# The last quarter of an MLP's second product, done as seven half-size products

## The chip, the cores and the metric

The kernel runs on one core of one Trainium2 chip. The time is that of the device, in microseconds, from one launch of the whole program: two layers of an encoder, each with a token mixer and an MLP. Only the MLPs are changed.

A core has a matrix engine (TensorE; PE in the profile, with its weight loads listed apart as PEld), a vector engine (DVE), a scalar engine (ACT), GpSimd (POOL), and a queue that issues transfers (SP). POOL can issue transfers too. Each engine works through its own list of instructions in order and waits on semaphores where it needs another engine's result. SBUF is the on-chip memory; PSUM is where TensorE writes.

## What is computed

The input is 512 tokens of 1024 float32 values. After each token mixer comes

```python
def _sq_relu_mlp(h, w1, w2):
    a = jax.nn.relu(jnp.matmul(h, w1))
    return jnp.matmul(a * a, w2)

x = _layernorm(DEEPNORM_ALPHA * x + _sq_relu_mlp(x, w1[i], w2[i]), ln2_g[i], ln2_b[i])
```

with `w1` 1024 x 4096 and `w2` 4096 x 1024, all float32. Layer 0 has a gated DeltaNet mixer in front of its MLP, layer 1 a gated linear attention mixer; layer 1's MLP writes the output.

## The kernel before

**Precision.** TensorE is used with operands rounded to a shorter format (`F32R`). Each float32 operand is split into a high part (a rounding copy on ACT, line 95) and a low part (source minus high part, on DVE, line 96). Every product is then three matmuls, high x high, high x low and low x high (`mm3`, lines 114 to 116). So a split of a block costs one ACT and one DVE operation, and a product of 128 x 128 by 128 x 512 costs three matmuls.

**Groups.** The MLP's 4096 hidden features are worked in four groups of 1024. The first product makes a group's hidden activations `h`, the second multiplies them with the group's 1024 rows of `w2` and adds the result to `x` (tiles `xt`, four of 128 tokens, each seen as two halves of 512 columns). While TensorE does the second product of group g, pieces of the first product of group g + 1 (`nxt()`) are placed between its parts, so that both kinds of matmul share the engine's list.

**Seven products.** For groups 0 to 2, function `second` (line 469) cuts the product into 2 x 2 blocks: tokens into two halves of 256, hidden features into two halves of 512 (`a11`, `a12`, `a21`, `a22`), and `w2` into four blocks of 512 x 512. A scheme of the Strassen-Winograd kind gives the result with seven block products in place of eight. Each of the seven is 24 matmuls (two token tiles, four slices of features, three matmuls each). It costs sums: of activation blocks on DVE, of weight blocks on DVE (`plus`, line 348), and more adds of PSUM banks into `x` (line 464), since some products go into two results. The `w2` blocks arrive in raw form in a ring of 8 tiles (`w2r`, 128 x 1024); their split parts live in rings of 3 (`w2h`, `w2l`), those of the activations in rings of 2 (`ah`, `al`).

**The last group.** Group 3 has no next group to mix with. Function `last` (line 539) does its second product plainly: eight `w2` pieces are loaded and split (`rows`), four blocks of activations are split (`part`), and then for each of the four token tiles and each half of the columns 8 x 3 matmuls go into one PSUM bank (`pl`), 192 matmuls in all. As soon as both halves of a token tile are added to `x`, its layernorm runs (`layernorm`, line 214; its `last=True` keeps all of it on DVE but for two tiny ACT operations). In layer 0 the tile is then transposed and split for the next mixer (`xpose`, line 168); in layer 1 it is stored to the output.

`layernorm` has a second form, with `sums`: row sums come from the adds into `x` themselves, the squares from two ACT operations (line 219), and with `last=False` one half of the final scaling goes to ACT (line 233) and POOL (line 234). The kernel before uses it only after the token mixers.

**Order.** The program is written in the order in which the work is meant to run; a framework places the instructions of each engine, inserts the semaphores and orders each engine's list by its own estimates of when operands are ready. The order is fixed when the program is built. A ring tile is given out again only when all its readers are done, so ring sizes and the order of use also bind the engines to each other.

Of the kernel before, what the change touches and what calls it, by code (L numbers as in the profile page):

```python
# [17 lines left out]
P = 128  # L18
# [10 lines left out]
class Ctx:  # L29
# [52 lines left out]
        return self.psum[tag].tile(list(shape), dt, name=name, tag=tag)  # L82


    def split(self, src, shape, pool=None):

        nc = self.nc
        if pool is None:
            hi = self.whl.tile(shape, F32R, name="wh", tag="wh")
            lo = self.whl.tile(shape, F32R, name="wl", tag="wl")  # L90
        else:
            pool, hi, lo, bufs = pool
            hi = pool.tile(shape, F32R, name=hi, tag=hi, bufs=bufs)
            lo = pool.tile(shape, F32R, name=lo, tag=lo, bufs=bufs)
        nc.scalar.copy(hi, src)  # L95
        nc.vector.tensor_tensor(lo, src, hi.bitcast(F32), ALU.subtract)  # L96
        return hi, lo

    def wcols(self, w, c0, n=P, pool=None):
# [202 lines left out]
def mlp(c, w1, w2, g, b, out=None, extra=None):  # L302
# [14 lines left out]
    with c.banks(pj=2, X=2, Y=2, Z=2), tc.tile_pool(name="mlp", bufs=2) as pool:  # L317
# [5 lines left out]
        def ring(name):  # L323
            return (pool, *RING[name])
# [8 lines left out]
        def load(gi, i, j):  # L333
            for q in range(2):
                blocks[i, j, q] = t = raw()
                r = (gi * GF + i * HF + 2 * q) * P
                c.dma(t, w2[r:r + 2 * P, 512 * j:512 * j + 512].rearrange("(k p) n -> p k n", p=P))

        def split(i):

            i_, j_ = {1: (0, 0), 2: (1, 0), 3: (1, 1), 4: (1, 0), 5: (0, 0), 6: (0, 0), 7: (0, 1)}[i]
            parts[i] = [c.split(blocks[i_, j_, q], [P, 2, 512], pool=ring("w2")) for q in range(2)]

            sums = {1: ((0, 0), (0, 1)), 2: ((0, 1), (1, 1)), 5: ((0, 0), (1, 1)), 6: ((1, 0), (0, 0))}
            if i in sums:
                plus(*sums[i])

        def plus(a, b):
# [106 lines left out]
        def pair(src, where="ah"):  # L455
            return c.split(src, [P, HF, HT], pool=ring(where))

        def add(t, hf, ps, op=ALU.add):
            xs = c.xh(t)[hf]
            if (t, hf) not in touched:  # L460
                touched.add((t, hf))
                V.scalar_tensor_tensor(xs, xs, ALPHA, ps, ALU.mult, op)
            else:
                V.tensor_tensor(xs, xs, ps, op)

        def quarters(h):
            return [h[j][:, :, HT * i:HT * i + HT] for i in range(2) for j in range(2)]

        def second(gi, h, a, nxt):

            a11, a12, a21, a22 = quarters(h)

            def banks(tag):
                return [c.bank([P, 512], F32, name="p" + tag, tag=tag) for _ in range(2)]

            def product(bk, a, i, new, by_tile=False):

                if i not in parts:
                    split(i)
                ws = parts.pop(i)  # L480
                order = [(q, j) for j in range(2) for q in range(2)] if by_tile else [(q, j) for q in range(2) for j in range(2)]
                for q, j in order:
                    wh, wl = ws[q]
                    sl = slice(j * P, (j + 1) * P)
                    for k in (2 * q, 2 * q + 1):
                        c.mm3(bk[j], a[0][:, k, sl], a[1][:, k, sl], wh[:, k % 2, :], wl[:, k % 2, :],
                              new and k == 0, k == HF - 1, skip_group_check=True)

            def fetch(i, j):
                if gi + 2 < G:  # L490
                    load(gi + 1, i, j)

            X, Y = banks("X"), banks("Y")
            load(gi, 1, 0)
# [32 lines left out]
                add(j, 1, Y[j], ALU.subtract)  # L527
            nxt()
            if gi + 2 == G:
                nxt()  # L530
                nxt()
            product(X, pair(a22), 4, False)
# [3 lines left out]
                nxt()  # L536
                nxt()

        def last(gi, h):

            par = c.load_ln(g, b, lambda i: pool.tile([P, 512], F32, name="ln", tag=("xh5", "xh6", "xl5", "xl6")[i], bufs=1))
            a, ws = {}, {}

            def part(i, j, home):
                a[i, j] = pair(h[j][:, :, HT * i:HT * i + HT], home)

            def rows(i, home=None):
                ws[i] = c.wrows(w2, (gi * GF + 2 * (i % 4)) * P, i // 4 * 512, pool=ring(home) if home else None)

            rows(0)  # L550
            rows(3, "w2")
            part(0, 0, "ah")
            rows(1)
            rows(2)
            part(0, 1, "raw")
            rows(4, "raw")
            rows(5, "raw")
            rows(6, "w2")
            rows(7, "w2")
            part(1, 0, "ah")  # L560
            part(1, 1, "raw")
            if out is None:
                c.new_x()
            for t in range(NT):
                sl = slice(t % 2 * P, t % 2 * P + P)
                for hf in range(2):
                    ps = c.bank([P, 512], F32, name="pl", tag="YZYZXZXZ"[2 * t + hf])
                    for k in range(GF):
                        wh, wl = ws[4 * hf + k // 2]
                        ah, al = a[t // 2, k // HF]  # L570
                        c.mm3(ps, ah[:, k % HF, sl], al[:, k % HF, sl], wh[:, k % 2, :], wl[:, k % 2, :], k == 0, k == GF - 1)
                    add(t, hf, ps)
                c.layernorm(c.xh(t), c.xh(t), par, last=True)
                if out is None:
                    c.xpose(t, c.xt[t], ("pj",))
                else:
                    nc.sync.dma_start(out[t * P:(t + 1) * P, :], c.xt[t])
# [31 lines left out]
        early = {}  # L609
        step = 0  # L610
        for gi in range(G - 1):
            more = gi + 2 < G
# [24 lines left out]
            second(gi, h, a, nxt)  # L637
            h, a = nh, nxt.a if more else None
        last(G - 1, h)


def sel_masks(c, pool, tmp):
# [992 lines left out]
```

## Time and profile before

| | us |
|---|---|
| median of 3 runs | 1374.56 (1373.52 to 1374.7) |
| the profiled execution | 1370.78 |
| its span in the trace | 1369.1 |
| TensorE busy (8317 matmuls) | 1341.5 |
| DVE busy | 1073.9 |
| ACT busy | 738.7 |
| POOL busy | 72.5 |
| last group of layer 0, first to last `pl` matmul | 721.8 to 769.9 |
| last group of layer 1, first to last `pl` matmul | 1315.5 to 1360.0 |

Rows of the profile read: start in us from the span's start, length in us, engine, line, operation, names (`out<-in`), shape, and in brackets the engine's idle time before it with what ended it. Group rows carry a count (x), total busy us and mean ns of one. Rows of windows give, for each engine, the busy time and the count of instructions within the stretch, then the granted TensorE clock, the share of DMA time and GB/s. Matmuls are pipelined: one shown with 0.39 us is followed by the next after about 0.23. Numbers behind tile names are left out, so `w2r<-w2r` is a sum of two weight blocks.

### The profile page before, as it was taken

The numbers are of one execution on the slowest core, as the hardware profiler recorded it, in microseconds if no ns is written. First come the engines' busy times: TensorE is split into PE (matmuls) and PEld (weight loads), VectorE is DVE, ScalarE is ACT, GpSimd is POOL, SyncE is SP. The second block draws the span as 40 slices with busy tenths as digits, with TensorE's granted clock in tenths as the row PEclk, the third lists the DMA queues.
The fourth block names the chain that finished last, engine by engine and source line by source line (L and its number), as shares of the span: only waits on it lengthen the run. The fifth ranks groups of instructions, "written<-read, shape, count | busy, mean of one in ns | idle before, by whom it ended". The sixth has DMA issues, their size and how long they took to land.

```text
span 1369.1 us, 21146 instructions
## 1 busy us (share of the span) xinstructions
PE 1341.5 (98%) x8317; PEld 1123.9 (82%) x8317; DVE 1073.9 (78%) x1685; ACT 738.7 (54%) x1444; POOL 72.5 (5%) x111
## 2 busy tenths in 40 slices
PE   8999999999999999999999999999999999999997
PEld 7777777777777888888887888888878888888886
DVE  7787787778677997897967687977779787979675
ACT  4776668765743655555553354654446455545440
POOL 5000000000003700000000000000000000000000
PEclk9999999999999999999999999999999999999999
DMA  6221112210251523243123332221325153322141
GB/s 190 63 62 48 47 32 63 60 35 32 78 154 57 176 78 108 77 154 93 47 90 100 91 92 76 62 62 62 99 55 185 47 154 92 124 78 60 47 152 49
DMA packets 145222, 117.44 MB, mean 86 GB/s; under 512 B 6571, under 2 KB 121379, under 8 KB 145123
## 3 DMA queue, kind: packets, MB, share of 16 engines
q1 hardware_dynamic: 143779, 111.90, 27.2%
q0 software_dynamic: 1344, 4.20, 1.1%
q8 instruction: 65, 1.06, 0.3%
q14 instruction: 34, 0.28, 0.1%
HBM read 113.99 MB, written 2.10 MB: 85 GB/s over the span
## 4 chain that ended last, share of the span: by engine, by line
PE 83%; ACT 7%; DVE 6%; DMA 2%; issue 1%; POOL 0%; DVEq 0%; SPq 0%; ACTq 0%
PE pj L115 5%; PE pj L116 5%; PE pj L114 5%; PE pX L114 3%; PE pX L115 3%; PE pX L116 3%; PE pjv L114 3%; PE pjv L115 3%; PE pjv L116 3%; PE fxz L114 2%; PE scp L865 2%; PE op L1561 2%; PE fxz L115 2%; PE fxz L116 2%; PE pl L115 2%; PE pl L116 2%
## 5 line engine op out<-in xcount | busy, mean ns | idle before, releaser
L95 ACT CAST wh<-wst 128x1024 fp32r<-128x1024 f32 x146 | 152.8, 1050 | 203.8 <-PE pj L115 49.8
L96 DVE TENSOR_TENSOR wl<-wst,wh 128x1024 fp32r<-128x1024 f32 x146 | 178.9, 1232 | 62.2 <-ACT wh L95 62.1
L115 PE MATMUL pj<-xtl,wh 128*128 128x512 f32 (+1 forms) x352 | 127.1, 361 | 0.5 <-DVE xtl L178 0.5
L114 PE MATMUL pj<-xth,wh 128*128 128x512 f32 (+1 forms) x352 | 126.8, 362 | 0.8 <-ACT xth L177 0.7
L116 PE MATMUL pj<-xth,wl 128*128 128x512 f32 (+1 forms) x352 | 126.7, 361 | 0.0
L96 DVE TENSOR_TENSOR w2l<-w2r,w2h 128x1024 fp32r<-128x1024 f32 x84 | 102.5, 1222 | 26.6 <-ACT w2h L95 26.5
L95 ACT CAST w2h<-w2r 128x1024 fp32r<-128x1024 f32 x84 | 88.2, 1050 | 64.5 <-PE pX L116 28.1
L114 PEld LDWEIGHTS pj<-xth,wh 128*128 128x128 f32 x352 | 66.2, 189 | 11.2 <-ACT xth L177 1.2
L115 PEld LDWEIGHTS pj<-xtl,wh 128*128 128x128 f32 x352 | 66.4, 189 | 10.9 <-DVE xtl L178 0.8
L115 PE MATMUL pX<-w2l,ah 128*128 128x512 f32 x192 | 75.0, 391 | 0.0
L116 PE MATMUL pX<-w2h,al 128*128 128x512 f32 x192 | 74.9, 390 | 0.0
L114 PE MATMUL pX<-w2h,ah 128*128 128x512 f32 x192 | 74.8, 393 | 0.0
L116 PEld LDWEIGHTS pj<-xth,wl 128*128 128x128 f32 x352 | 66.4, 189 | 10.2
L95 ACT CAST ah<-h 128x1024 fp32r<-128x1024 f32 x46 | 48.4, 1053 | 46.8 <-PE pX L115 20.8
L351 DVE TENSOR_TENSOR w2r<-w2r 128x1024 f32<-128x1024 f32 x48 | 58.1, 1233 | 0.3
L96 DVE TENSOR_TENSOR al<-h,ah 128x1024 fp32r<-128x1024 f32 x46 | 56.2, 1221 | 0.6
L114 PE MATMUL pjv<-wh,xth 128*128 128x512 f32 x128 | 54.7, 427 | 0.0
L116 PE MATMUL pjv<-wh,xtl 128*128 128x512 f32 x128 | 50.2, 392 | 0.0
L115 PE MATMUL pjv<-wl,xth 128*128 128x512 f32 x128 | 50.0, 390 | 0.0
L116 PEld LDWEIGHTS pX<-w2h,al 128*128 128x128 f32 x192 | 36.1, 188 | 7.5
L116 PE MATMUL pjk<-xth,wl 128*128 128x512 f32 (+1 forms) x112 | 41.8, 373 | 0.0
L114 PEld LDWEIGHTS pX<-w2h,ah 128*128 128x128 f32 x192 | 35.8, 188 | 7.1 <-ACT w2h L95 0.3
(469 smaller groups left out, 3915.4 us busy)
## 6 DMA issues: line engine op xcount, KB each, us to landing
wst<-in_mlp_w SPq DMA_DIRECT2D x80, 512.0 KB, 4.3
w2r<-in_mlp_w SPq DMA_DIRECT2D x48, 512.0 KB, 3.7
wst<-in_a_w_in SPq DMA_DIRECT2D x32, 512.0 KB, 4.1
wst<-in_b_w_in SPq DMA_DIRECT2D x32, 256.0 KB, 3.0
wst<-in_a_w_out SPq DMA_DIRECT2D x8, 512.0 KB, 3.8
wst<-in_b_w_in SPq DMA_DIRECT2D x8, 512.0 KB, 3.8
wst<-in_b_w_out SPq DMA_DIRECT2D x8, 512.0 KB, 3.6
xt<-in_x SPq DMA_DIRECT2D x4, 512.0 KB, 4.1
```

Of the source, the lines that this page charges most:

```text
L95: nc.scalar.copy(hi, src)
L96: nc.vector.tensor_tensor(lo, src, hi.bitcast(F32), ALU.subtract)
L114: mm(ps, ah, bh, start=start, stop=False, **kw)
L115: mm(ps, ah, bl, start=False, stop=False, **kw)
L116: mm(ps, al, bh, start=False, stop=stop, **kw)
L351: V.tensor_tensor(blocks[a + (q,)], blocks[a + (q,)], blocks[b + (q,)], ALU.add)
L865: T.matmul(ps[:, n, :], kh[:, sl], qh[:, sl], start=True, stop=True)
L1561: T.matmul(op[:, n, :], l, r, start=i == 0, stop=i == len(mm) - 1)
```

## The change

Group 3 is now done with the seven products too. `last` takes the split first block of activations `a`, as `second` does, and runs the products in the order 1, 5, 2, 6, 3, 7, 4, with nothing between them. Three things differ from `second`:

- The sums of weight blocks are no DVE operations. `plus` issues transfers from POOL that read one raw tile in SBUF and add it to another (`accum_op=ALU.add`), 128 x 1024 each, two for each of four sums: eight per layer.
- Of each weight block's two halves, the first (q = 0) is split as before. The second gets tiles of its own (`xh3`/`xl3` and `xh7`/`xl7`, free since the first product's last use), and its low part is computed on POOL. That holds for products 2 to 7 of the group; product 1's halves are split on ACT and DVE ahead of time.
- The layernorm of token tiles 0 to 2 uses the `sums` form. That of tile 3 uses the old form in layer 1 and the `sums` form in layer 0. The output is stored in halves of 512 columns. Products 3, 7 and 4 finish one token tile before they start on the other (`by_tile`), and in layer 0 the transposes of tiles 0 and 1 stand within product 4 (`behind`).

Around it: the first block of group 3 is split within group 2's loop (`split(1)`), `w2` of group 3 is fetched within group 2's products (`fetch` without its condition), and group 2's product 4 is split before the last two pieces of the first product instead of after. POOL's instructions within `last` are held in the order in which they are written (`in_order`). `banks` and `product` move out of `second` unchanged but for the `behind` hook.

```diff
-    def split(self, src, shape, pool=None):
+    def split(self, src, shape, pool=None, lo_on=None):
...
-        nc.vector.tensor_tensor(lo, src, hi.bitcast(F32), ALU.subtract)
+        (lo_on or nc.vector).tensor_tensor(lo, src, hi.bitcast(F32), ALU.subtract)
...
-        def split(i):
+        def split(i, homes=None):
...
-            parts[i] = [c.split(blocks[i_, j_, q], [P, 2, 512], pool=ring("w2")) for q in range(2)]
+            parts[i] = [c.split(blocks[i_, j_, q], [P, 2, 512], *((homes if homes and q else (ring("w2"),))))
+                        for q in range(2)]
...
-                plus(*sums[i])
+                plus(*sums[i], homes)
...
-                V.tensor_tensor(blocks[a + (q,)], blocks[a + (q,)], blocks[b + (q,)], ALU.add)
+                if by_dma:
+                    nc.gpsimd.dma_start(blocks[a + (q,)], blocks[b + (q,)], accum_op=ALU.add)
+                else:
+                    V.tensor_tensor(blocks[a + (q,)], blocks[a + (q,)], blocks[b + (q,)], ALU.add)
...
             if gi + 2 == G:
+                split(4)
                 nxt()
                 nxt()
...
-        def last(gi, h):
+        def last(gi, h, a):
+            homes = {i: ((pool, f"xh{k}", f"xl{k}", 1), nc.gpsimd) for i, k in ((5, 3), (2, 7), (6, 3), (3, 7), (7, 3), (4, 7))}
+            a11, a12, a21, a22 = quarters(h)
...
+            def full(t, hf, ps, sign=1.0):
+                xs = c.xh(t)[hf]
+                V.scalar_tensor_tensor(xs, ps, sign, xs, ALU.mult, ALU.add, accum_out=sums[t][:, hf:hf + 1])
+
+            def norm(t, end):
+                if end and out is not None:
+                    c.layernorm(c.xh(t), c.xh(t), par, end)
+                else:
+                    junk = pool.tile([P, HF, S], F32, name="h", tag="h", bufs=3)
+                    c.layernorm(c.xh(t), c.xh(t), par, end, (sums[t], (junk[:, 0, :], junk[:, 1, :])))
+                if out is not None:
+                    for q in range(2):
+                        nc.sync.dma_start(out[t * P:(t + 1) * P, 512 * q:512 * q + 512], c.xh(t)[q])
...
+            load(gi, 1, 0)
+            X, Y = banks("Z"), banks("Y")
+            V.tensor_tensor(a21, a22, a21, ALU.subtract)
+            a5 = pair(a21)
+            split(5, homes[5])
+            product(X, a, 1, True)
+            for j in range(2):
+                add(j, 0, X[j])
+            a2 = pair(a12)
+            split(2, homes[2])
+            product(Y, a5, 5, True)
+            V.scalar_tensor_tensor(a11, a21, -1.0, a11, ALU.mult, ALU.subtract)
+            V.scalar_tensor_tensor(a21, a11, -1.0, a22, ALU.mult, ALU.subtract)
+            for j in range(2):
+                add(2 + j, 1, Y[j], ALU.subtract)
+            a6 = pair(a11)
+            split(6, homes[6])
+            Z = banks("X")
+            product(Z, a2, 2, True)
+            V.scalar_tensor_tensor(a12, a12, -1.0, a11, ALU.mult, ALU.subtract)
+            for j in range(2):
+                full(j, 0, Z[j])
+            a3 = pair(a12)
+            split(3, homes[3])
+            product(X, a6, 6, False)
+            for j in range(2):
+                add(j, 1, X[j], ALU.subtract)
+            a7 = pair(a21)
+            split(7, homes[7])
+            product(Y, a3, 3, False, True)
+            for j in range(2):
+                full(j, 1, Y[j], -1.0)
+            a4 = pair(a22, "raw")
+            split(4, homes[4])
+            product(X, a7, 7, False, True)
+            for j in range(2):
+                full(2 + j, 1, X[j], -1.0)
+            norm(0, False)
+            norm(1, False)
+            product(X, a4, 4, False, True, turn)
+            for j in range(2):
+                full(2 + j, 0, X[j])
+                norm(2 + j, j == 1)
+            turn(2)
+            turn(3)
...
-                if half == 1 and i % 4 == 2 and more:
-                    split(1)
+                if half == 1 and i % 4 == 2:
+                    split(1, None if i + 2 < len(todo) else (None, None))
                     nxt.a = pair(quarters(nh)[0])
...
-        last(G - 1, h)
+        with c.in_order(mybir.EngineType.Pool):
+            last(G - 1, h, a)
```

The lines numbered in the prediction are those of the kernel before, except line 556, which is the `scalar_tensor_tensor` within `full` of the changed kernel.

More of the change, by code (lines that the diff above doesn't have):

```diff
@@ L537, in second @@
                 nxt()
-        def last(gi, h):
+        def last(gi, h, a):
+            homes = {i: ((pool, f"xh{k}", f"xl{k}", 1), nc.gpsimd) for i, k in ((5, 3), (2, 7), (6, 3), (3, 7), (7, 3), (4, 7))}
+            a11, a12, a21, a22 = quarters(h)
             par = c.load_ln(g, b, lambda i: pool.tile([P, 512], F32, name="ln", tag=("xh5", "xh6", "xl5", "xl6")[i], bufs=1))
[L542 to L561, printed above, removed]
+            sums = [c.small.tile([P, 2], F32, name="lns", tag="lns") for t in range(NT)]
@@ L562, in last @@
             if out is None:
                 c.new_x()
[L564 to L573, printed above, removed]
+            def full(t, hf, ps, sign=1.0):
+                xs = c.xh(t)[hf]
+                V.scalar_tensor_tensor(xs, ps, sign, xs, ALU.mult, ALU.add, accum_out=sums[t][:, hf:hf + 1])
@@ L574, in last, with turn @@
+            def turn(t):
                 if out is None:
                     c.xpose(t, c.xt[t], ("pj",))
-                else:
-                    nc.sync.dma_start(out[t * P:(t + 1) * P, :], c.xt[t])
+            load(gi, 1, 0)
[7 more added lines that the diff above has]
+            a2 = pair(a12)
@@ L611, in mlp @@
         for gi in range(G - 1):
-            more = gi + 2 < G
             nh = new_h()
```

35 lines of the change are left out of this document (18 added, 17 removed).

## The prediction

> **What bounds the kernel now.** I read the page first (busy shares and the chain that ended last), then the stretch of the second layer's last group by windows, then the timelines of PE and DVE there.
>
> ```profile
> PE 1341.5 (98%) x8317; PEld 1123.9 (82%) x8317; DVE 1073.9 (78%) x1685; ACT 738.7 (54%) x1444; POOL 72.5 (5%) x111
> ...
> PE 83%; ACT 7%; DVE 6%; DMA 2%; issue 1%; POOL 0%; DVEq 0%; SPq 0%; ACTq 0%
> ```
>
> TensorE is busy nearly always and carries 83% of the chain; GpSimd (POOL) is almost unused. The windows show the second layer before its last group, then that group's first 11 us and the rest of its matmuls:
>
> ```profile
> 1280.00:1315.00 35.00, 35.00 (x194) 30.43 (x193) 19.86 (x25) 16.79 (x23) 2.15 (x4) 1.00 0.32 107
> 1315.00:1326.00 11.00, 10.74 (x46) 8.13 (x45) 10.12 (x10) 8.12 (x10) 0.00 (x0) 1.00 0.38 139
> 1326.00:1360.00 34.00, 33.64 (x148) 27.89 (x149) 20.36 (x42) 1.50 (x6) 0.00 (x0) 1.00 0.11 47
> ```
>
> Behind the stretch and its length stand the busy times of PE, the weight loads, DVE, ACT and POOL. PE is full. DVE is full only for the 11 us in which the splits are made; it works 19.9 of the 35 us before and 20.4 of the 34 after. So fewer matmuls pay one for one, as long as what replaces them fits on DVE.
>
> ```profile
> 1256.63 0.39 PE L114 MATMUL pY<-w2h,ah 128*128 128x512 f32 x1
> ...
> 1261.85 0.39 PE L116 MATMUL pY<-w2h,al 128*128 128x512 f32 x1
> ...
> 1315.51 0.39 PE L114 MATMUL pl<-wh,ah 128*128 128x512 f32 x1
> ...
> 1326.36 0.50 PE L115 MATMUL pl<-w2l,w2r 128*128 128x512 f32 x1 [0.61 <-DVE w2l L96]
> ```
>
> The first two rows are the ends of one seven-product product of 24 matmuls: (1261.85 - 1256.63) / 23 = 0.227 us each, so 5.45 us a product. The last two are the group at stake: its first matmul at 1315.51 (called T0 below) and its one wait, of 0.61 us.
>
> **The change part by part.**
>
> *Matmuls.* 192 become 7 x 24 = 168. 24 x 0.227 = 5.45 us a layer, and the wait of 0.61 goes with its order: -6.1 us in each of two layers, all of it on PE's path.
>
> *What DVE has to do instead.* Each product needs a split of its own weight block and of its own activations. In the built program's order DVE has, between the finished activations and the add that frees product 4's bank (line 556 for token tile 2): 16 operations of 128x1024 on two SBUF tiles (four sums of activation blocks, six low parts of activations, six of weights), 13 adds of a PSUM bank into x, and the first part of tile 0's layernorm.
>
> ```profile
> 1318.57 0.68 DVE L464 TENSOR_TENSOR xt<-xt,pX 128x512 f32<-128x512 f32 x1
> 1319.17 1.22 DVE L96 TENSOR_TENSOR w2r<-wst,w2r 128x1024 fp32r<-128x1024 f32 x1
> 1320.30 1.22 DVE L96 TENSOR_TENSOR al<-h,ah 128x1024 fp32r<-128x1024 f32 x1
> ...
> 1329.52 0.75 DVE L226 SCALAR_TENSOR_TENSOR xt<-xt,bmv,ln 128x512 f32<-128x512 f32 x1
> ...
> 1330.92 0.15 DVE L189 SCALAR_TENSOR_TENSOR rst<-bmv,rst 128x1 f32<-128x1 f32 x1
> ```
>
> By the distance of the starts a 128x1024 operation costs 1.13 us and a PSUM add 0.60. 16 x 1.13 = 18.1; 13 x 0.60 = 7.8; the layernorm part is three operations of 128x512 like line 226 (0.7 from start to start) and seven of one column (0.15): 3.2. Together 29.1 us, while PE needs 6 x 5.45 = 32.7 us to reach product 4. That alone would fit.
>
> *GpSimd's half of the low parts.* Six 128x1024 subtractions go to POOL. The trace shows what such an operation does to DVE:
>
> ```profile
> 21.73 1.29 POOL L1073 TENSOR_TENSOR off<-blk 128x512 f16<-128x512 f32 x1
> ...
> 423.81 1.71 POOL L234 TENSOR_TENSOR xt<-xt,lnp 128x512 f32<-128x512 f32 x1 [27.80 <-ACT xt L233]
> 427.23 1.27 POOL L234 TENSOR_TENSOR xt<-xt,lnp 128x512 f32<-128x512 f32 x1 [1.71 <-ACT xt L233]
> ```
>
> ```profile
> 21.75 2.35 DVE L96 TENSOR_TENSOR wl<-wst,wh 128x1024 fp32r<-128x1024 f32 x1
> ...
> 423.62 0.74 DVE L231 SCALAR_TENSOR_TENSOR xt<-xt,rstd,lnp 128x512 f32<-128x512 f32 x1
> 424.28 1.26 DVE L189 SCALAR_TENSOR_TENSOR rst<-bmv,rst 128x1 f32<-128x1 f32 x1
> ...
> 427.10 0.68 DVE L178 TENSOR_TENSOR xtl<-tp,xth 128x512 fp32r<-128x512 f32 x1
> ```
>
> The split at 21.75 began 20 ns after a POOL operation of 1.29 us and took 2.35 in place of 1.22: it lost 1.13 us, all but 0.16 of POOL's time. At 423.81 POOL had to wait for line 231 (1.71 in place of 1.27), and then a one-column DVE operation waited for POOL (1.26 us in place of 0.15). The line 178 operation, with one operand in PSUM, ran beside POOL at its usual 0.68. So in this trace POOL and a DVE operation on two SBUF tiles exclude each other for the whole operation, and PSUM adds are exempt.
>
> ```profile
> L1083 POOL TENSOR_TENSOR ic<-ic 128x64 f32<-128x64 f32 x1 | 0.3, 324 | 0.1
> ```
>
> From 324 ns at 64 columns to 1.27 us at 512, undisturbed, is 2.11 ns a column: 2.35 us at 1024, an estimate. Each then takes 2.35 - 0.16 = 2.2 us from DVE, twice what DVE would need for the same split. Five of the six fall into the stretch counted above: 11.0 us. A pair of adds beneath one hides 1.2. Bounds for DVE's work: 29.1 + 11.0 - 5 x 1.2 = 34.1 with adds beneath all five, 40.1 with none. In the built order adds stand next to some of them, and I take two covered: 37.7. DVE also waits for ScalarE, whose casts and squares feed it in order: I add 2 us, three of the squares below, with 0 to 3 as bounds. Work starts when the last activation is squared:
>
> ```profile
> 1315.67 0.63 ACT L450 ACTIVATE h<-h 128x512 f32<-128x512 f32 x1
> ```
>
> This ended at T0 + 0.8; with two weight casts fewer ahead of it I expect it 2 us earlier, and after the first POOL operation DVE starts at about T0 - 1.5. So the add of tile 2 ends at -1.5 + 37.7 + 2 = T0 + 38.2, and PE, due at T0 + 32.7, has lost 5.5 us (bounds -0.1, which is nothing, and 8.9), spread over the products as late low parts. The matmuls saved are given back here.
>
> *Product 4's second half, and the tail (layer 1).* The add for tile 3 stands on DVE behind tile 1's layernorm and a POOL addition of 128x512 (3.2 + 1.27 against the 2.7 us of a half product): 1.2 us of waiting, 0 to 2. At the end DVE still holds most of tile 2's layernorm when PE finishes, where before only tile 3's was left:
>
> ```profile
> 1360.46 0.69 DVE L464 TENSOR_TENSOR xt<-xt,pl 128x512 f32<-128x512 f32 x1 [4.02 <-PE pl L116]
> ```
>
> Then it waited 4.02 us for PE; now PE's end finds it busy. Tile 2's 3.2 us and one POOL addition fall between, less what has run by then: +2.3 (0.5 to 4). Storing in halves saves perhaps 0.2, within that.
>
> *Layer 0.* The same -6.1 + 5.5. Transposes of tiles 0 and 1 fill product 4's wait, but the layernorms of tiles 1 to 3 follow the last matmul instead of one, and the next token mixer's first projection waits for them:
>
> ```profile
> 771.14 0.36 PE L114 MATMUL pjq<-xth,wh 128*128 128x256 f32 x1 [0.87 <-DVE xt L464]
> ```
>
> Before, that wait was 0.87 us because other tokens came first. I take two layernorm parts and one POOL addition on PE's path, less 2.7 us of work that it has meanwhile: 2 x 3.2 + 1.27 - 2.7 = +5.0 (1 to 7).
>
> *Accumulating transfers.* Eight per layer stand for what would be eight sums on DVE. No row shows an accumulating transfer.
>
> ```profile
> w2r<-in_mlp_w SPq DMA_DIRECT2D x48, 512.0 KB, 3.7
> ...
> wst<-in_b_w_in SPq DMA_DIRECT2D x32, 256.0 KB, 3.0
> ...
> lnp<-in_ln_b POOLq DMA_DIRECT2D x2, 256.0 KB, 3.4
> ```
>
> ```profile
> DMA to landing us min/median/max: 3.3/5.2/7.4
> ```
>
> 256 KB more cost 0.7 us on SP's queue, so 512 KB move in 1.4 of 3.7; POOL's queue adds 0.4. If each byte must be read, read again and written, 3.4 - 0.7 + 2 x 1.4 = 5.5 us; bounds are the second view's 3.3 and 7.4, the row of the layernorm loads from POOL. ScalarE casts product 6's block ahead of product 2's activations, so the second sum, issued near T0 + 1.7, must have landed by about T0 + 7.5: 5.8 us are hidden, and 7.4 would cost 1.6 us a layer. I take nothing. The Trainium skill, "DMA: Bandwidth & Descriptors", section "Anatomy of one DMA — SWDGE (gpsimd) path", gives 2.0 us plus bytes / 436e3 per transfer, an estimate of 3.2 us for 512 KB, so nothing is exposed by it either; for 256 KB it would be 2.6, and the trace disagrees (3.4).
>
> Sum: layer 0 -6.1 + 5.5 + 5.0 = +4.4; layer 1 -6.1 + 5.5 + 1.2 + 2.3 = +2.9. The splits for product 1 and the earlier split of product 4 put three low parts more (3.4 us) on DVE before T0, where it has 15 us to spare: 0.1 us a layer, up to 3.4 if that cover were gone. Together +7.5. The profiled execution took 1370.78 us, 3.78 under the median of the runs; it would become 1378.3, and on the median's scale 1374.56 + 7.5 = 1382.
>
> **The rivals.**
>
> *DVE keeps up (the other side).* If a POOL operation cost DVE little, its 29.1 us would start at -1.5, with 2 of waiting, and end before 32.7. Then both layers keep 6.1, less about 1 us each of later tail: -10.2, 1364. For it: DVE's slack of 14 us between 1326 and 1360. Against: the row of 2.35 us. It decides at a loss of about 1.0 us per POOL operation: 3.1 / 5 = 0.6 uses up the slack, and 1.9 us more in each layer, with the tails above, eat the gain. The Trainium skill, "SBUF — State Buffer", section "SBUF: two separate sides", has the port pair as an exclusive lock held for the whole instruction; by that rule this rival falls, and the trace agrees at 21.75.
>
> *Slow accumulation.* Beyond 5.8 us each microsecond costs one or two per layer, through ScalarE's queue and GpSimd's order: 8 us gives 1382 + 7 = 1389, 10 us about 1396. For it: the landings up to 7.4 us of POOL's transfers, though those ran beside weight loads.
>
> *The gain and the stalls cancel.* Adds beneath all five POOL operations (3.6 us a layer less) bring 1382 - 7.2 = 1375.
>
> **How the numbers follow.** Within 0.2% (2.7 us) is about what a measurement of this kernel tells from no change. Forecast (DVE bound, 1377 to 1390) 0.52; slow accumulation (1389 to 1405) 0.14; cancelling 0.08; DVE keeps up (1361 to 1371) 0.26. Faster 0.27, same 0.07, slower 0.66. The range 1364 to 1392 leaves out half of the second and a third of the last case.
>
> **What would show it.** PE waits of 0.5 to 3 us for low parts of line 96 in products 2 to 7; DVE operations of over 3 us beside POOL subtractions of 2.3 to 2.5 us; a wait at product 4's start for line 556; accumulating transfers of 4 to 6 us. If DVE's splits stay at 1.2 us beside POOL, or PE shows no wait in this group, the forecast is wrong and the time is near 1364.

## The result, and the profile after

The change makes the kernel slower: 1384.03 us (median of 5 runs, 1380.82 to 1385.62) against 1374.7 us (1373.52 to 1376.9) for the kernel before, run on the same chip. The ratio is 1.0063, 95% interval 1.0045 to 1.0081, so 6 to 11 us. The profiled execution took 1383.11 us (span 1381.4). Predicted were 1382, with 1364 to 1392 as range.

The page of the changed kernel: busy times, the chain that ended last by engine, three groups of instructions, and the transfers that sum blocks.

```profile
PE 1339.8 (97%) x8269; PEld 1121.0 (81%) x8269; DVE 1105.9 (80%) x1714; ACT 769.8 (56%) x1496; POOL 126.9 (9%) x145
...
PE 67%; DVE 12%; issue 11%; ACT 8%; DMA 1%; POOL 0%; DVEq 0%; POOLq 0%; ACTq 0%
...
L96 DVE TENSOR_TENSOR w2l<-w2r,w2h 128x1024 fp32r<-128x1024 f32 x98 | 127.9, 1307 | 27.3 <-ACT w2h L95 27.3
...
L96 DVE TENSOR_TENSOR al<-h,ah 128x1024 fp32r<-128x1024 f32 x54 | 70.5, 1306 | 0.6
L353 POOL DMA_DIRECT2D w2r<-w2r x16 | 15.0, 1099 | 486.8 <-DVE w2l L96 264.7
...
w2r<-w2r POOLq DMA_DIRECT2D x16, 512.0 KB, 5.8
```

TensorE has fewer matmuls (8269 against 8317) and carries less of the chain, 67% against 83%. DVE's share of the chain doubled, but ten of the sixteen points that TensorE lost went to "issue" (1% before), time for which the profile shows no reason. These shares alone do not explain the loss: the run with one input on GpSimd below, faster than the kernel before, has the very same line. POOL is busy 54 us longer and DVE 32. The mean low part takes 1307 and 1306 ns where it took 1222 and 1221 before, which is about 13 of the 32 us; most of the rest are splits that are new (98 and 54 in place of 84 and 46). The kernel before:

```profile
L96 DVE TENSOR_TENSOR w2l<-w2r,w2h 128x1024 fp32r<-128x1024 f32 x84 | 102.5, 1222 | 26.6 <-ACT w2h L95 26.5
...
L96 DVE TENSOR_TENSOR al<-h,ah 128x1024 fp32r<-128x1024 f32 x46 | 56.2, 1221 | 0.6
```

In the second layer's last group, the timeline of POOL and then that of DVE:

```profile
1326.78 3.07 POOL L96 TENSOR_TENSOR xl<-w2r,xh 128x1024 fp32r<-128x1024 f32 x1
...
1336.92 3.16 POOL L96 TENSOR_TENSOR xl<-w2r,xh 128x1024 fp32r<-128x1024 f32 x1 [5.35 <-ACT xh L95]
...
1345.18 2.39 POOL L96 TENSOR_TENSOR xl<-w2r,xh 128x1024 fp32r<-128x1024 f32 x1 [3.39 <-ACT xh L95]
1349.56 2.48 POOL L96 TENSOR_TENSOR xl<-w2r,xh 128x1024 fp32r<-128x1024 f32 x1 [1.99 <-ACT xh L95]
...
1358.89 2.39 POOL L96 TENSOR_TENSOR xl<-w2r,xh 128x1024 fp32r<-128x1024 f32 x1 [6.85 <-ACT xh L95]
```

```profile
1327.37 3.58 DVE L96 TENSOR_TENSOR w2l<-w2r,w2h 128x1024 fp32r<-128x1024 f32 x1
...
1337.74 1.28 DVE L468 TENSOR_TENSOR xt<-xt,pY 128x512 f32<-128x512 f32 x2
1338.94 2.22 DVE L96 TENSOR_TENSOR w2l<-w2r,w2h 128x1024 fp32r<-128x1024 f32 x1
...
1345.58 3.07 DVE L96 TENSOR_TENSOR al<-h,ah 128x1024 fp32r<-128x1024 f32 x1
...
1349.71 3.42 DVE L96 TENSOR_TENSOR w2l<-w2r,w2h 128x1024 fp32r<-128x1024 f32 x1
...
1359.44 1.86 DVE L217 SCALAR_TENSOR_TENSOR bmv<-lns,bias 128x1 f32<-128x1 f32 x1
```

Each DVE operation with both operands in SBUF that starts beside a POOL subtraction waits for its end: 3.42 in place of 1.22 us at 1349.71, and 1.86 us for a one-column operation (0.22 without POOL). The pair of adds at 1337.74, which read PSUM, keeps its 1.28 us, although POOL is at work from 1336.92 to 1340.08.

TensorE's rows of that group that begin with a wait of 0.3 us or more, headed by the group's first matmul:

```profile
1323.94 0.39 PE L114 MATMUL pZ<-w2h,ah 128*128 128x512 f32 x1
...
1342.35 0.50 PE L116 MATMUL pZ<-w2h,al 128*128 128x512 f32 x1 [1.01 <-DVE al L96]
1348.71 0.50 PE L116 MATMUL pY<-w2h,al 128*128 128x512 f32 x1 [0.58 <-DVE al L96]
1355.51 0.50 PE L116 MATMUL pZ<-w2h,al 128*128 128x512 f32 x1 [0.94 <-DVE al L96]
1363.39 0.50 PE L114 MATMUL pZ<-w2h,w2r 128*128 128x512 f32 x1 [2.58 <-DVE xt L556]
1366.80 0.50 PE L114 MATMUL pZ<-w2h,w2r 128*128 128x512 f32 x1 [0.35 <-DVE xt L556]
```

Every wait is for DVE: low parts of line 96, then the adds of line 556 that free product 4's banks.

The best single view for this change is a window from the last matmul of the activations (`fxz`) to the last matmul of all, and from there to the end. First the kernel before, then the changed one; behind stretch and length stand the busy times of PE, the weight loads, DVE, ACT and POOL.

```profile
1311.29:1360.04 48.75, 48.13 (x213) 39.12 (x211) 31.84 (x52) 12.06 (x19) 0.00 (x0) 1.00 0.24 89
1360.04:1369.10 9.06, 0.38 (x2) 0.00 (x0) 4.87 (x11) 0.50 (x2) 0.00 (x0) 0.70 0.14 58
```

```profile
1319.71:1369.43 49.72, 44.09 (x189) 34.31 (x187) 44.44 (x58) 24.08 (x36) 23.38 (x14) 1.00 0.39 84
1369.43:1381.40 11.97, 0.39 (x2) 0.00 (x0) 8.29 (x20) 2.48 (x9) 1.55 (x1) 0.63 0.34 131
```

There are 24 matmuls fewer, yet the stretch is 1.0 us longer, and the tail behind it 2.9 us. DVE works 44.4 of the 49.7 us where it worked 31.8. Layer 1 loses 3.9 us. In layer 0 the way from the last `fxz` or `fy` matmul to the next mixer's first gate projection (`gps`) went from 60.66 to 65.90 us, by the starts of those matmuls: 5.2 us. Together 9.1, close to the 9.3 between the medians. The two profiled executions differ by 12.3 us; about 3.5 of them arise in the first 40 us of the program, which the change does not touch, so the executions are compared by these stretches.

### The profile page after: what moved, and what is told of

It is laid out like the page before. It is cut to its first block, busy times and chain, and to the rows that moved or that the text cites. A ratio compares the mean times of both kernels' runs of the same rounds, so it can differ in the third digit from the quotient of the medians.

```text
span 1381.4 us, 21220 instructions
## 1 busy us (share of the span) xinstructions
PE 1339.8 (97%) x8269; PEld 1121.0 (81%) x8269; DVE 1105.9 (80%) x1714; ACT 769.8 (56%) x1496; POOL 126.9 (9%) x145
## 4 chain that ended last, share of the span: by engine, by line
PE 67%; DVE 12%; issue 11%; ACT 8%; DMA 1%; POOL 0%; DVEq 0%; POOLq 0%; ACTq 0%
PE pj L115 5%; PE pj L116 5%; PE pj L114 5%; PE pX L114 3%; PE pX L115 3%; PE pX L116 3%; PE pjv L114 2%; PE pjv L115 2%; PE pjv L116 2%; PE op L1600 2%; PE fxz L114 2%; DVE w2l L96 2%; PE fxz L116 2%; PE fxz L115 2%; ACT wh L95 2%
## 5 line engine op out<-in xcount | busy, mean ns | idle before, releaser
L95 ACT CAST wh<-wst 128x1024 fp32r<-128x1024 f32 x140 | 146.5, 1050 | 189.6 <-PE pj L115 48.1
L96 DVE TENSOR_TENSOR wl<-wst,wh 128x1024 fp32r<-128x1024 f32 x140 | 171.6, 1233 | 51.9 <-ACT wh L95 50.8
L96 DVE TENSOR_TENSOR w2l<-w2r,w2h 128x1024 fp32r<-128x1024 f32 x98 | 127.9, 1307 | 27.3 <-ACT w2h L95 27.3
L95 ACT CAST w2h<-w2r 128x1024 fp32r<-128x1024 f32 x98 | 102.9, 1050 | 74.7 <-PE pX L116 28.1
L95 ACT CAST ah<-h 128x1024 fp32r<-128x1024 f32 x54 | 56.8, 1052 | 51.1 <-PE pX L115 20.9
L116 PE MATMUL pX<-w2h,al 128*128 128x512 f32 x200 | 78.2, 391 | 0.7 <-DVE al L96 0.7
L114 PE MATMUL pX<-w2h,ah 128*128 128x512 f32 x200 | 77.9, 393 | 0.0
L114 PEld LDWEIGHTS pj<-xth,wh 128*128 128x128 f32 x352 | 66.2, 189 | 11.2 <-ACT xth L177 1.2
L116 PEld LDWEIGHTS pj<-xth,wl 128*128 128x128 f32 x352 | 66.4, 189 | 10.2
L96 DVE TENSOR_TENSOR al<-h,ah 128x1024 fp32r<-128x1024 f32 x54 | 70.5, 1306 | 0.6
L353 POOL DMA_DIRECT2D w2r<-w2r x16 | 15.0, 1099 | 486.8 <-DVE w2l L96 264.7
L116 PE MATMUL pjv<-wh,xtl 128*128 128x512 f32 x128 | 50.2, 392 | 0.0
L116 PE MATMUL pY<-w2h,al 128*128 128x512 f32 x112 | 44.4, 396 | 2.6 <-DVE al L96 2.6
```

What stands on the lines that cost most here:

```text
L96: (lo_on or nc.vector).tensor_tensor(lo, src, hi.bitcast(F32), ALU.subtract)
L114: mm(ps, ah, bh, start=start, stop=False, **kw)
L116: mm(ps, al, bh, start=False, stop=stop, **kw)
L353: nc.gpsimd.dma_start(blocks[a + (q,)], blocks[b + (q,)], accum_op=ALU.add)
```

## Experiments

Theory: DVE is the bound of the last group, because every subtraction on POOL shuts DVE out for its whole length. Rivals: the accumulating transfers are late; the new form of layernorm makes the tails; ScalarE's casts stand in a bad order. Each kernel was timed over five rounds against the kernel before on the same chip. Ratios are to the kernel before; the change itself is 1.0063. An edit can also make the framework order the engines' lists anew, so that more than the edited step differs.

### Low parts on DVE

```
-  (lo_on or nc.vector).tensor_tensor(lo, src, hi.bitcast(F32), ALU.subtract)
+  nc.vector.tensor_tensor(lo, src, hi.bitcast(F32), ALU.subtract)
```

> The change with every low part on DVE; GpSimd computes none. Exclusion theory (a GpSimd subtraction holds DVE for 2.2 us where DVE itself needs 1.13): DVE's work per layer falls by about 5 x (2.2 - 1.13) less covered adds, 3 us, so 1384 becomes about 1378, ratio to before 1.003 (1.000 to 1.005). Rival, late accumulating transfers: no change, 1.006. Rival, GpSimd's work is free for DVE: DVE gets 5.6 us more a layer, 1395, ratio 1.014.

Measured: 1.0037 (1.0023 to 1.0051), near the theory's 1.003. DVE does six splits more per layer, and the kernel gets faster than with GpSimd's help, though the two intervals overlap and the lists of DVE and ScalarE are in another order. TensorE's one large wait left in layer 1 is for a cast. ScalarE's row of it and the one that TensorE needed:

```profile
1336.27 1.04 ACT L95 CAST w2r<-h 128x1024 fp32r<-128x1024 f32 x1 [7.18 <-DMA w2r<-w2r]
1337.22 1.04 ACT L95 CAST ah<-h 128x1024 fp32r<-128x1024 f32 x1
```

```profile
1338.32 0.50 PE L114 MATMUL pZ<-w2h,ah 128*128 128x512 f32 x1 [2.16 <-ACT ah L95]
```

The first cast makes product 4's activations, needed last; its tile (a `w2r` slot) is free only when an accumulating transfer has read it. Product 6's cast stands behind it.

### Low parts as copies on ScalarE

```
+  if lo_on is not None:
+      nc.scalar.copy(lo, src)
+  else:
+      nc.vector.tensor_tensor(lo, src, hi.bitcast(F32), ALU.subtract)
```

> GpSimd's low parts are replaced by a copy on ScalarE, which leaves out the subtraction (0.95 us each, neither GpSimd nor DVE works on them). Exclusion theory: DVE's 29 us fit, the 5.5 us of waits in the products vanish in each layer, so 1384 becomes about 1373, ratio 0.998 to 1.000, with the later tails still there. Rival, transfers: 1.006 stays. Rival, tails alone: 1.006 stays.

Measured: 1.0001 (0.9991 to 1.0011). With the six low parts off both DVE and POOL the loss is gone, but there is no gain: the same cast again waited for a transfer, and the tail stayed at 11.7 us. What each of the two cost was not run by itself. ScalarE's row:

```profile
1331.08 1.05 ACT L95 CAST w2r<-h 128x1024 fp32r<-128x1024 f32 x1 [6.51 <-DMA w2r<-w2r]
```

### No sums of weight blocks

```
   for q in range(2):
-      if by_dma:
-          nc.gpsimd.dma_start(blocks[a + (q,)], blocks[b + (q,)], accum_op=ALU.add)
-      else:
+      if not by_dma:
```

> The eight accumulating transfers of each last group are left out (so the weight-block sums are missing); everything else as in the change. Exclusion theory: they are hidden, 1382 to 1384, ratio 1.005 to 1.006. Rival, transfers: the 5.8 us landings are on the path, 1376 or less, ratio 1.000 or less.

Measured: 1.0042 (1.0028 to 1.0055). That is a little under the theory's 1.005 to 1.006 and far from the rival's 1.000. Two thirds of the loss stay without a single accumulating transfer, so they are not the main cause. The difference to the change, 0.0021 or some 2.9 us, is an upper hint of what the transfers and their issue on POOL cost; the two intervals overlap.

### The sums of weight blocks on DVE

```
-  if by_dma:
+  if False:
```

> The change with the sums of weight blocks on DVE in place of accumulating transfers. Exclusion theory: DVE is the bound, so six sums of 1.13 us a layer inside the group add 6.8 us a layer, 1397, ratio 1.016 (1.010 to 1.020). Rival, transfers: a sum on DVE is ready sooner than a landing of 5.8 us, so no slower than the change, 1.006 or less.

Measured: 1.0088 (1.0073 to 1.0103), less than expected by this theory and more than by its rival. DVE's sums in and ahead of layer 1's last group:

```profile
1314.29 1.22 DVE L355 TENSOR_TENSOR w2r<-w2r 128x1024 f32<-128x1024 f32 x1
1316.56 1.22 DVE L355 TENSOR_TENSOR w2r<-w2r 128x1024 f32<-128x1024 f32 x1
1323.09 3.40 DVE L355 TENSOR_TENSOR w2r<-w2r 128x1024 f32<-128x1024 f32 x1 [3.08 <-POOL xl L96]
1331.01 1.21 DVE L355 TENSOR_TENSOR w2r<-w2r 128x1024 f32<-128x1024 f32 x1
1342.43 2.35 DVE L355 TENSOR_TENSOR w2r<-w2r 128x1024 f32<-128x1024 f32 x2
```

I had counted six of the eight in the crowded stretch. Four came before its start at 1320.64 (two more, at 1296.71, stand ahead of these rows), where DVE had room. That leaves four, about 4.5 us in place of 6.8. Why the loss against the change is smaller still was not run. So the transfers are worth having, by some 3 us (0.0025, with intervals that overlap), far less than the DVE time that they replace.

### The old form of layernorm

```
-  if end and out is not None:
-      c.layernorm(c.xh(t), c.xh(t), par, end)
+  if True:
+      c.layernorm(c.xh(t), c.xh(t), par, last=True)
```

> The change with the old form of layernorm (statistics, scaling and shift all on VectorE) for all four token tiles of the last group, so GpSimd has no additions there and ScalarE no squares. Per tile VectorE does about 4.6 us in place of 3.2 plus a GpSimd addition of 1.3 to 1.6 that excludes it. My theory (the tails are VectorE's backlog, whichever form it has): no difference beyond 1.5 us to the change, ratio to the kernel before 1.005 to 1.008. Rival (the new form and GpSimd's additions make the tails, 2.3 us in layer 1 and most of 5.0 in layer 0): about 5 us less than the change, 1.002 to 1.004.

Measured: 1.0088 (1.0069 to 1.0106). Neither side: by the medians it is 2 us slower than the change, by the ratios 3.4, with intervals that overlap. The rows of layer 1, to the last matmul and to the end:

```profile
1323.10:1374.90 51.80, 45.22 (x188) 35.52 (x187) 47.76 (x65) 19.45 (x26) 20.64 (x12) 0.97 0.40 89
1374.90:1385.70 10.80, 0.39 (x2) 0.00 (x0) 7.47 (x20) 0.86 (x4) 0.00 (x0) 0.65 0.25 97
```

DVE has 55.2 us of work in place of 52.7 (44.44 + 8.29). The tail is 1.2 us shorter, but the stretch before is 2.1 us longer. The new form is not what makes the loss.

### One input on GpSimd

```
+  if lo_on is not None:
+      nc.gpsimd.tensor_copy(lo, src)
+  else:
+      nc.vector.tensor_tensor(lo, src, hi.bitcast(F32), ALU.subtract)
```

> The six GpSimd low parts of each last group become GpSimd copies of one input of the same shape (the subtraction is left out of the computation). Theory that any GpSimd operation on SBUF excludes a VectorE operation on two SBUF tiles: VectorE operations of over 2.2 us stand beside the copies as before, each lengthened by the part of the copy that it overlaps; the time is that of the change less what a shorter copy gives back, ratio 1.003 to 1.008. Rival (only GpSimd operations with two inputs take the shared path): all VectorE low parts keep 1.22 us and the ratio is 1.000 to 1.002, like the run with ScalarE copies.

Measured: 0.9971 (0.9960 to 0.9983): faster than the kernel before, and below what either side expected. It leaves the subtraction out, so it measures a price and is no version to keep. A copy on POOL, and the three DVE operations of layer 1's last group that stand beside one:

```profile
1335.39 1.04 POOL L97 CAST xl<-w2r 128x1024 fp32r<-128x1024 f32 x1 [1.70 <-PE pX L118]
```

```profile
1322.04 2.19 DVE L99 TENSOR_TENSOR w2l<-w2r,w2h 128x1024 fp32r<-128x1024 f32 x1
...
1335.51 2.00 DVE L99 TENSOR_TENSOR w2l<-w2r,w2h 128x1024 fp32r<-128x1024 f32 x1 [0.93 <-ACT w2h L95]
...
1340.92 2.08 DVE L99 TENSOR_TENSOR w2l<-w2r,w2h 128x1024 fp32r<-128x1024 f32 x1
```

The exclusion is there with one input too (2.00 in place of 1.22 us), so the rival falls. But the copy is over in 1.04 us where the subtraction takes about 2.4 at best. The loss per operation drops from up to 2.4 to between 0.8 and 1.0 us, and with it every wait of TensorE in layer 1's products but one of 0.39 us. The length of POOL's operation is the price, as the theory has it; that it depends so much on the number of inputs I had not known.

This is the cleanest of the runs. TensorE, DVE and ScalarE have the same instructions in the same order as in the change, in the last groups of both layers; only POOL's operations are shorter. In layer 1 the DVE rows beside POOL are longer by 2.6 us in all, where the change has 9.1, and the stretch to the last matmul takes 42.9 us in place of 49.7.

The Trainium skill, "GPSIMD Engine Reference", section "3.1 Elementwise — side-by-side cycle accounting", has 2.6 cycles an element for two inputs as a limit of the read port and 1.03 for the simplest loops. At the 1.2 GHz that it uses, that is an estimate of 2.2 and 0.88 us for 1024 columns; the trace agrees within a fifth, with 2.39 and 1.04.

### The change with its casts in order

```
-  with c.in_order(mybir.EngineType.Pool):
+  with c.in_order(mybir.EngineType.Pool), c.in_order(mybir.EngineType.Activation):
       last(G - 1, h, a)
```

> The change, with ScalarE's instructions of the last group held in the order in which the code writes them; GpSimd keeps its low parts. In the change the cast of product 4's activations stood at 1341.20 after 4.36 us of waiting, ahead of a weight cast that TensorE needed at once (wait of 1.40 us). Theory that VectorE with GpSimd's exclusion is the bound: what is won there is lost at the next products, at most 2 us less, ratio 1.005 to 1.007. Rival (order of the casts as cause of the stalls): 3 to 6 us less, ratio 1.002 to 1.004.

Measured: 1.0056 (1.0039 to 1.0073), as the theory had it. With POOL's subtractions in place the order of the casts is not the bound. In layer 1 the products end 3.1 us sooner than in the change, but the tail takes back 1.7 (table below); the theory had put that at the next products.

### Low parts on DVE, casts in order

The same edit together with the first one.

> Low parts all on VectorE, and ScalarE's instructions of the last group held in the order in which the code writes them. In the run with low parts on VectorE alone, the built order had the cast of product 4's activations ahead of the casts for product 6; it waited for an accumulating transfer until 1336.3, and TensorE stood 2.55 and 0.93 us behind it, in layer 0 about 2.5. Theory (that cast's place is the cause): these waits go, 3 to 6 us less than 1.0037, ratio 0.999 to 1.002. Rival (VectorE's 36 us of work against 32.7 us is the bound whatever the casts do): waits of the same sum come back at later products, ratio 1.003 to 1.004.

Measured: 1.0021 (1.0010 to 1.0031). In part: the cast was the cause of the wait, but a tail took over much of the gain. Layer 1 in windows:

```profile
1314.50:1356.58 42.08, 42.08 (x189) 34.85 (x187) 38.16 (x57) 22.79 (x32) 5.92 (x7) 1.00 0.43 86
1356.58:1373.10 16.52, 0.39 (x2) 0.00 (x0) 12.08 (x28) 4.90 (x14) 3.49 (x3) 0.59 0.33 127
```

The 2.55 and 0.93 us of the expectation are distances between the starts of two matmuls; as waits they are 2.16 and 0.53 in layer 1 of that run. Here TensorE is busy for all of 42.08 us: no wait is left in the products, and they end 6.7 us sooner after the last `fxz` than in the kernel before. Then it has nothing to do for 16.5 us in place of 9.1, while layernorm is worked off.

### Casts in order, layernorm free

```
-  with c.in_order(mybir.EngineType.Pool), c.in_order(mybir.EngineType.Activation):
+  with c.in_order(mybir.EngineType.Pool):
       last(G - 1, h, a)
   ...
   def last(gi, h, a):
       ...
+      with c.in_order(mybir.EngineType.Activation):
           load(gi, 1, 0)
           ...
           product(X, a7, 7, False, True)
```

> Low parts all on VectorE and ScalarE's casts of the last group in the order of the code, but the squares and scalings of layernorm left free to be placed. In the run before this, with layernorm held in order too, TensorE finished the second layer's matmuls 42.1 us after the last activation product (48.7 in the kernel before) and the tail behind it was 16.5 us (9.0): tile 2's squares, ready at 1355.3, stood behind tile 1's scaling until 1361.6, and in layer 0 TensorE waited 4.18 us for a transposed tile whose copy stood behind tile 1's scaling. Theory (these places in the queue are what is left): the tail of layer 1 is 12 to 13.5 us and the wait in layer 0 below 2 us, so 4 to 6 us less than 1.0021: 0.997 to 0.999. Rival (VectorE's amount of work sets the end, and a matmul saved is a longer tail): 1.001 to 1.003.

Measured: 0.9994 (0.9984 to 1.0004), no difference to the kernel before.

```profile
1314.54:1356.62 42.08, 42.08 (x189) 34.85 (x187) 38.84 (x60) 23.80 (x36) 5.25 (x6) 1.00 0.44 90
1356.62:1371.50 14.88, 0.39 (x2) 0.00 (x0) 11.22 (x25) 3.66 (x11) 4.42 (x3) 0.62 0.36 141
```

The tail is 1.6 us shorter, not 3 to 4.5 as expected, and in layer 0 TensorE's wait for the transposed tile is still 2.02 us. DVE is busy for 11.2 us of the tail without a gap, and the rest is the last store, 3.5 us as in the kernel before. In the time the theory was nearly right (its range ended at 0.999); in the tail the rival was: there DVE's amount of work sets the end.

### The form of layernorm, on top of that

All four tiles in the old form; then the two tiles that finish last; then the new form with its last step on DVE alone:

```
+  if True:      (all four)   /   if t > 1:      (the two that come last)
+      c.layernorm(c.xh(t), c.xh(t), par, last=True)

-  c.layernorm(c.xh(t), c.xh(t), par, end, (sums[t], (junk[:, 0, :], junk[:, 1, :])))
+  c.layernorm(c.xh(t), c.xh(t), par, True, (sums[t], (junk[:, 0, :], junk[:, 1, :])))
```

> As the run with casts in order and layernorm free, with the old form of layernorm (all on VectorE) for all four tiles. It puts about 1.4 us more on VectorE per tile for three tiles per layer, and takes GpSimd's additions of 1.3 to 1.6 us away. Theory (VectorE and what excludes it set the end): within 1.5 us of that run, 0.997 to 1.001. Rival (chains through ScalarE and GpSimd make the tails): 2 to 4 us less than that run, 0.995 to 0.997.

> As the run with casts in order and layernorm free, with the old form of layernorm for the two tiles that come last and the new one for the two that finish earlier, under matmuls. Theory: the tail of layer 1 is shorter than with either form for all (tile 2 has no squares to wait for, 10.5 to 12 us), 0.996 to 0.999. Rival (VectorE's amount alone counts): the same as with one form for all, within 1 us.

> As the run with casts in order and layernorm free, with the last step of layernorm's second half for three tiles per layer as one VectorE operation of 0.67 us in place of ScalarE's scaling and GpSimd's addition; ScalarE's squares stay. In that run the three additions in layer 1 held VectorE up by 0.53, 1.00 and 1.06 us, 2.6 together; three operations of 0.67 are 2.0. Theory (exclusion on VectorE, which is the bound of the tails): 0.6 to 1.5 us less per layer, ratio 0.997 to 0.999. Rival (the two have the same price, or the chain through ScalarE is what ends last): within 0.5 us per layer, 0.999 to 1.000.

Measured: 1.0027 (1.0016 to 1.0038), 1.0004 (0.9994 to 1.0014) and 0.9990 (0.9978 to 1.0001). The first was expected at 1.001 or less and missed: more work on DVE, more time, 2.9 us of it in layer 0. The second moved nothing that can be told, and its theory missed too: layer 1's tail is 14.2 us, not 10.5 to 12. The third took POOL's last additions off DVE's way and is the best that keeps all of the computation; its interval still touches no change. It gained 1.0 us in layer 1, as its theory had it, and 0.2 in layer 0, as the rival had it.

### All runs by their two stretches

From the starts of the matmuls named above, in us. The sixth column is the sum of the differences to the kernel before in layer 0 (to `gps`) and layer 1 (both stretches); the seventh is the ratio less one times 1374.

| | layer 0 to `gps` | layer 1 to last matmul | tail | DVE busy, layer 1 | both, to before | by the ratio |
|---|---|---|---|---|---|---|
| before | 60.7 | 48.8 | 9.1 | 36.7 | | |
| the change | 65.9 | 49.7 | 12.0 | 52.7 | +9.1 | +8.7 |
| low parts on DVE | 64.1 | 46.8 | 13.4 | 49.3 | +5.8 | +5.1 |
| low parts as ScalarE copies | 60.2 | 46.4 | 11.7 | 42.9 | -0.2 | +0.1 |
| no sums | 65.1 | 47.0 | 12.0 | 51.7 | +5.5 | +5.8 |
| sums on DVE | 66.4 | 48.9 | 14.5 | 55.4 | +11.3 | +12.1 |
| old layernorm | 68.3 | 51.8 | 10.8 | 55.2 | +12.5 | +12.1 |
| one input on GpSimd | 60.1 | 42.9 | 12.0 | 45.8 | -3.5 | -4.0 |
| change, casts in order | 64.9 | 46.6 | 13.7 | 54.1 | +6.7 | +7.7 |
| low on DVE, casts in order | 62.9 | 42.1 | 16.5 | 50.2 | +3.0 | +2.9 |
| the same, layernorm free | 60.6 | 42.1 | 14.9 | 50.1 | -0.9 | -0.8 |
| all old layernorms | 63.5 | 42.1 | 15.6 | 52.3 | +2.7 | +3.7 |
| two old layernorms | 61.5 | 42.1 | 14.2 | 50.3 | -0.6 | +0.5 |
| no GpSimd additions | 60.4 | 42.1 | 13.9 | 49.4 | -2.1 | -1.4 |

The two stretches account for each ratio to within about 1 us. Where DVE is busy for 49 us or more, layer 1's total (the second and third columns together) is DVE's busy time and 5 to 11 us, however it is divided between waits of TensorE and the tail. That spread is as large as most of the differences, so this is a loose relation.

## Why the prediction was right, point by point

In layer 1 each term can be read from the rows, and the mechanism holds. In layer 0 the total came out near, but in part by other terms than those of the sum.

**Matmuls, -6.1 a layer.** Right in layer 1: 48.75 to 42.08 us, -6.7, in each run where nothing else stopped TensorE. In layer 0 transposes stand among the matmuls, so the term cannot be read there.

**GpSimd's half of the low parts, 2.2 us of DVE each.** Shown. Undisturbed, the subtraction took 2.39 to 2.41 us in layer 1 (estimate 2.35); 3.42 us beside 1.22 is the 2.2 us. Beside layer 1's five operations in the stretch the DVE rows are longer by 2.4, 1.0, 1.9, 2.2 and 1.6 us, 9.1 in all, against 11.0 less the two covered pairs, 8.6. Adds from PSUM were exempt, as assumed. The point at which this decides, put at 1.0 us per operation, stood between the two prices that were run: 2.2 gave 1.0063, about 0.9 gave 0.9971.

**DVE frees product 4's bank at T0 + 38.2.** By the rows above TensorE began it at 1363.39 - 1323.94 = 39.5 in layer 1. In layer 0 it was 767.20 - 725.67 = 41.5, 3.3 us later than predicted. That term, 5.5 us, was thus 6.8 and 8.8. POOL's subtractions lengthen DVE's rows of layer 0 by much the same as in layer 1, 9.9 us. What the sum leaves out for layer 0 are three splits of the next mixer's weights, about 2.5 us, that DVE does in the same stretch:

```profile
744.43 0.28 DVE L155 TENSOR_TENSOR wh<-gst,wh 128x128 fp32r<-128x128 f32 x1
744.63 1.21 DVE L96 TENSOR_TENSOR wl<-wst,wh 128x1024 fp32r<-128x1024 f32 x1
...
756.66 1.21 DVE L96 TENSOR_TENSOR wl<-wst,wh 128x1024 fp32r<-128x1024 f32 x1
```

The 2 us for waiting on ScalarE were 1.8 in layer 1: 0.88 for squares, as the prediction says, and 0.92 for a weight cast. That cast came late because the cast for the last product was placed ahead of it and waited, here for a low part on DVE:

```profile
1341.20 1.04 ACT L95 CAST w2r<-h 128x1024 fp32r<-128x1024 f32 x1 [4.36 <-DVE w2l L96]
```

With POOL's subtractions in place its position costs little (1.0056 against 1.0063).

**Product 4's second half, +1.2, and the tail, +2.3.** Measured 0.4 of waiting (row at 1366.80) and 2.9 (11.97 - 9.06). The prediction's own terms for the first, 3.2 + 1.27 less 2.7, give 1.8, not 1.2; both are too much.

**Layer 0, +5.0 after the last matmul.** From the last matmul to `gps` the way went from 8.4 to 12.3 us, +4.0, so the size is about right. The mechanism is not: the prediction has TensorE waiting there for layernorms, and it waited 1.8 us in place of 0.9. The other 3 us or so are work: 16 transposes and 7 projection matmuls more now stand behind the last matmul. That the number is near is in part luck. The stretch up to the last matmul is 1.3 us longer, although those transposes have left it:

```profile
717.59:769.88 52.29, 51.61 (x236) 41.35 (x235) 37.89 (x62) 17.94 (x29) 0.00 (x0) 1.00 0.29 89
```

```profile
721.45:775.03 53.58, 47.66 (x196) 37.55 (x195) 49.25 (x65) 28.19 (x44) 23.91 (x14) 0.94 0.42 96
```

The granted clock is 0.94 where it was 1.00 before, which the prediction does not have. After a wait of 2.00 us TensorE's matmuls are (754.30 - 751.74) / 6 = 0.43 us apart in place of 0.23:

```profile
751.16 0.79 PE L116 MATMUL pY<-w2h,al 128*128 128x512 f32 x1 [2.00 <-DVE al L96]
751.74 0.63 PE L114 MATMUL pY<-w2h,ah 128*128 128x512 f32 x1
...
754.30 0.55 PE L114 MATMUL pY<-xh,ah 128*128 128x512 f32 x1
```

The same comes after the wait of 2.85 us ahead of product 4, for eight matmuls; at 0.2 us each that is an estimate of 1.6 us on TensorE's path. The wait of 2.58 us in layer 1 was not followed by it, so what sets it off stays open. The run with one input on GpSimd has 1.00 in both layers, so part of its gain in layer 0 is this; in layer 1 none is. Layer 0's total was 5.2 against +4.4, layer 1's 3.9 against +2.9.

**Accumulating transfers at nothing.** Size right: 5.8 us in the median (estimate 5.5). The cast of layer 1 that waited longest for one began at T0 + 6.4, within the 7.5 that the prediction allows, and DVE had no gap there:

```profile
1330.33 1.05 ACT L95 CAST w2h<-w2r 128x1024 fp32r<-128x1024 f32 x1 [4.26 <-DMA w2r<-w2r]
```

That all of it was hidden may still be too kind: without the transfers the kernel was 2.1 thousandths faster, about 2.9 us, part of which may be POOL's issuing. The intervals overlap, and the exact price stays open.

**The rivals.** That DVE keeps up came nearest to true with copies on POOL, 4 us faster than before where that rival has 10, and not with subtractions. Slow accumulation as the main cause fell with the run without sums. That the change would cancel itself is what the repaired versions do, though not for that rival's reason: the saved matmuls become a longer tail. What I missed is that taking GpSimd out would not restore the gain: DVE's work alone then eats it.

## What to carry to other kernels

Where one engine is full, fewer instructions on it pay only if the engine that feeds it has room in that very stretch, its tail included; add up the feeder's work to the end of the stretch before counting the saving. Work handed to GpSimd to relieve DVE cost DVE in these runs what was left of GpSimd's operation whenever DVE's operands were both in SBUF (3.42 us in place of 1.22 beside a subtraction, 2.00 beside a copy): compare that length, not its own engine's idle time, with what DVE would need. And in a list that is worked in order, a cast that is needed last but placed early can hold all those behind it.

## What the runs showed that I had not expected

GpSimd's one-input copy of 128 x 1024 is over twice as fast as its subtraction (1.04 against 2.39 us), and shuts DVE out just the same.

In two runs that differ in this, the accumulating transfers that were issued closer together landed later: the change issues them in pairs (1325.62, 1329.65 and 1340.03 in layer 1), the run with low parts on DVE and casts in order issues four in 3.57 us from 1322.65. Their time from issue to landing, as shortest, median and longest, in the change and then in that run:

```profile
DMA to landing us min/median/max: 4.5/5.8/8.2
```

```profile
DMA to landing us min/median/max: 4.5/7.2/11.6
```

In the second neither TensorE nor ScalarE waited for one of them in the last groups, so landings of up to 11.6 us (in layer 0; 10.8 in layer 1) were hidden once no cast stood ahead of its turn.
